# A Strassen scheme (seven block products for eight) for the gate and up projections of a decoder's FFN on one core

## The chip, the cores and the metric

The kernel runs on one core of a Trainium2 chip. The metric is device microseconds (us) of one execution, the median of several. The engines are named as the profile names them: PE (TensorE, the matmuls; PEld is its weight load), DVE (VectorE), ACT (ScalarE), POOL (GpSimd) and SP (which here only issues DMAs). PSUM is the memory that PE writes, SBUF the one that everything else lies in.

## The reference

One inference step of a two-layer decoder for 512 prompt tokens and 64 sample tokens, 576 columns in all, model width 1024. The change is in the FFN that closes each layer:

```python
D_MODEL = 1024
D_FF = -(-8 * D_MODEL // (3 * 256)) * 256        # 2816
def rmsnorm(x, g): ...
a = rmsnorm(x, norm_ffn[l])
x = x + (silu(a @ w_ffn_gate[l]) * (a @ w_ffn_up[l])) @ w_ffn_down[l]
```

Everything is float32.

## The kernel before

The activations stay in SBUF, features on the partitions: `h` is 8 chunks of 128 features by 576 columns. float32 accuracy is had from float32r matmuls by splitting: each operand is a high part H (ScalarE copies it to float32r) and a low part L (the remainder, subtracted on VectorE or GpSimd). A product W·X is three matmuls, WH·XH, WH·XL and WL·XH, added up in PSUM.

Weights come in blocks of 256 output columns by up to 8 chunks (`wblock`): two DMAs of 512 KB into `raw`, ACT writes `wh`, DVE or POOL (in turns, `remainder`, L303 and L305) writes `wl`. `dense` makes the next block while PE works on this one.

In the FFN the 576 columns are cut in 256 and 320. For the 256 the tile class `Halves` lays H and L side by side, so that WH·XH and WH·XL are one matmul of 512 columns (L239), followed by one of 256 for WL·XH (L241); `gather` (L222, L223) adds the two halves of PSUM up. The 320 take three matmuls (L235 to L237). `norm` makes the operand, chunk by chunk, while the matmuls of `dense` on `w_mem_o` are still adding to `h` (L374 `add_h`); 1/rms is multiplied onto the results later (`rs`, L284).

`ffn` goes through the 22 chunks of the hidden width in three groups of 8, 7 and 7. In a group, for each pair of chunks, a gate block (L284, L1043 Silu, L1044) and an up block (L1049, L1051, L1052) are made, which leave the operand `f` of the down projection; then `w_ffn_down` is applied to the group. So there are 11 gate and 11 up blocks of 256 columns in a layer, 44 in the kernel; here "block" always means one of these.

A framework turns the Python order into one instruction stream for each engine, puts semaphores where data or buffers ask for it, and shifts instructions by a plan of its own. On each engine they start in the order of the stream.

Of the kernel before, what the change touches and what calls it, by code (L numbers as in the profile page):

```python
# [94 lines left out]
def hybrid_step(ctx: ExitStack, tc: tile.TileContext, off, a, o):  # L95
# [104 lines left out]
    class Halves:  # L200
        def __init__(self, nm):
            self.t = [BIG(nm + x, FR) for x in "01"]

        def hl(self, c):
            return self.t[c // 4][:, 0:2048].rearrange("p (c x n) -> p c x n", x=2, n=256)[:, c % 4]

        def H(self, c, s0):
            return self.t[c // 4][:, 2048 + c % 4 * 320:2368 + c % 4 * 320] if s0 else self.hl(c)[:, 0]

        def L(self, c, s0):  # L210
            return self.t[c // 4][:, 3328 + c % 4 * 320:3648 + c % 4 * 320] if s0 else self.hl(c)[:, 1]

    both = [False]

    def bank(M, X, s0, n):
        p = ACC()
        return p[:M] if isinstance(X, Halves) and s0 == 0 and both[0] else p[:M, :n]

    def gather(po, n):
        if po.shape[1] > n:  # L220
            t = TMP("lo")[:po.shape[0], :n]
            nc.scalar.activation(t, po[:, n:n * 2], AF.Copy)  # L222
            last[0] = nc.vector.tensor_add(po[:, 0:n], po[:, 0:n], t)  # L223
        return po[:, 0:n]

    def products(po, W, X, k, ms, s0, n, nk):
        WH, WL = W[0][:, k, ms], W[1][:, k, ms]
        if isinstance(X, tuple):
            H, L = (x[:, k, s0:s0 + n] for x in X)
            nc.tensor.matmul(po, WH, H, start=k == 0, stop=False)  # L230
            nc.tensor.matmul(po, WH, L, start=False, stop=False)  # L231
            nc.tensor.matmul(po, WL, H, start=False, stop=k == nk - 1)  # L232
        elif po.shape[1] == n:
            H = X.H(k, s0)
            nc.tensor.matmul(po, WH, H, start=k == 0, stop=False)  # L235
            nc.tensor.matmul(po, WH, X.L(k, s0), start=False, stop=False)  # L236
            nc.tensor.matmul(po, WL, H, start=False, stop=k == nk - 1)  # L237
        else:
            nc.tensor.matmul(po.rearrange("p (x n) -> p x n", x=2), WH, X.hl(k), start=k == 0, stop=False,  # L239
                             skip_group_check=True)  # L240
            nc.tensor.matmul(po[:, 0:n], WL, X.H(k, 0), start=False, stop=k == nk - 1, skip_group_check=True)  # L241

    rs, rv, ssq = {}, {}, {}

    def norm(nm, l):
        X = Halves("a")
        for s0, n in HV:
            ssq[s0] = smp.tile([128, 320], FT, tag="ssq", name="ssq", bufs=2)[:, :n]
        for b in range(4):
            for s0, n in HV:  # L250
                s = slice(s0, s0 + n)
                acc = ssq[s0]
                for c in range(2 * b, 2 * b + 2):
                    g = vec(nm, l * 8 + c)
                    H = X.H(c, s0)
                    nc.scalar.activation(H, h[:, c, s], AF.Copy, scale=g)
                    nc.vector.scalar_tensor_tensor(X.L(c, s0), h[:, c, s], g, H, op0=OP.mult, op1=OP.subtract)  # L257
# [8 lines left out]
        normed[0] = X  # L266
        return X
# [22 lines left out]
    def plain(hi, lo, x):  # L290
        return [(hi, lo, x)]
# [15 lines left out]
    def wblock(w, k0, nk, m0, mc, load=None, order=None, into=None):  # L307
        WH, WL = into or [wp.tile([128, 8, 256], FR, tag=x, name=x) for x in ("wh", "wl")]
        for kk in range(0, nk, 4):
# [7 lines left out]
            remainder(WH[:, kk:kk + n, :mc], WL[:, kk:kk + n, :mc], raw[:, :n, :mc], order, into)  # L317
# [10 lines left out]
    def dense(w, X, k0, nk, m0, ncols, ev, load=None, order=None, fill=None, nxt=None, tick=None, hold=None):  # L328
        late = None
        W = ready.pop() if ready else wblock(w, k0, nk, m0, min(256, ncols), load, order)  # L330
        for b0 in range(0, ncols, 256):
            mc = min(256, ncols - b0)
            W0 = W
# [5 lines left out]
            for s0, n in HV:  # L339
                for mm in range(0, mc, 128):  # L340
# [3 lines left out]
                    if hold is not None and b0 == 0:  # L344
                        for k in range(nk - 1):
                            products(po, W0, X, k, ms, s0, n, nk)
                            pump(hold, 1)
# [6 lines left out]
                    if X is normed[0]:  # L354
                        rstd_cols(s0)
# [1501 lines left out]
```

## Time and profile before

| | us |
|---|---|
| median of 3 runs | 2116.62 (2116.26 to 2122.13) |
| the profiled execution, its own time | 2111.78 |
| its span, first to last instruction | 2109.9 |
| PE busy in the span | 2018.5 (96%) |
| DVE, ACT, POOL busy | 1111.7, 865.6, 801.0 |
| mean granted clock of PE | 0.984 of full |

A matmul's duration in a row runs from its start to its modelled end, and the next one starts long before that, so what a matmul costs is read from start to start. The two FFN stages are the stretches 596 to 1017 us and 1675.6 to 2099.7 us.

### The profile page before, as it was taken

The numbers are of one execution on the slowest core, as the hardware profiler recorded it, in microseconds if no ns is written. First come the engines' busy times: TensorE is split into PE (matmuls) and PEld (weight loads), VectorE is DVE, ScalarE is ACT, GpSimd is POOL, SyncE is SP. The second block draws the span as 40 slices with busy tenths as digits, with TensorE's granted clock in tenths as the row PEclk, the third lists the DMA queues.
The fourth block names the chain that finished last, engine by engine and source line by source line (L and its number), as shares of the span: only waits on it lengthen the run. The fifth ranks groups of instructions, "written<-read, shape, count | busy, mean of one in ns | idle before, by whom it ended". The sixth has DMA issues, their size and how long they took to land. (4 is left out here: it accounts for less than half of the span.)

```text
span 2109.9 us, 35813 instructions
## 1 busy us (share of the span) xinstructions
PE 2018.5 (96%) x14105; PEld 1817.6 (86%) x14105; DVE 1111.7 (53%) x2012; ACT 865.6 (41%) x1817; POOL 801.0 (38%) x752
## 2 busy tenths in 40 slices
PE   7999988999999999999969999999899999999998
PEld 6989846977899999999969977778887999999998
DVE  5478886544443333334535777765544433333344
ACT  5354555444333233133324547665444433232341
POOL 5354583422244234144302335563421443242342
PEclk9999998999999999999989999999999999999999
DMA  6545133255422222223344122312354222223232
GB/s 233 162 155 164 56 126 101 81 180 169 137 81 81 80 81 82 89 66 101 99 133 143 48 73 76 94 48 57 130 180 160 81 80 80 80 75 97 80 117 113
DMA packets 211156, 225.01 MB, mean 107 GB/s; under 512 B 13527, under 2 KB 191767, under 8 KB 210917
## 3 DMA queue, kind: packets, MB, share of 16 engines
q1 hardware_dynamic: 210989, 222.73, 33.0%
q8 instruction: 111, 1.82, 0.3%
q14 instruction: 56, 0.46, 0.1%
HBM read 210.04 MB, written 17.08 MB: 108 GB/s over the span
## 5 line engine op out<-in xcount | busy, mean ns | idle before, releaser
L235 PE MATMUL acc<-a,wh 128*128 128x320 f32 (+2 forms) x1616 | 501.4, 310 | 2.5 <-DVE hpb L500 2.5
L237 PE MATMUL acc<-a,wl 128*128 128x320 f32 (+2 forms) x1616 | 490.2, 303 | 0.0
L236 PE MATMUL acc<-a,wh 128*128 128x320 f32 (+2 forms) x1616 | 489.6, 303 | 0.0
L301 ACT ACTIVATE wh<-raw 128x1024 fp32r<-128x1024 f32 (+2 forms) x270 | 259.9, 986 | 384.1 <-PE acc L236 183.3
L305 POOL TENSOR_TENSOR wl<-raw,wh 128x1024 fp32r<-128x1024 f32 (+2 forms) x100 | 228.5, 2288 | 373.4 <-ACT wh L301 367.9
L235 PEld LDWEIGHTS acc<-a,wh 128*128 128x128 f32 (+1 forms) x1616 | 306.0, 189 | 9.4 <-issue 3.3
L236 PEld LDWEIGHTS acc<-a,wh 128*128 128x128 f32 (+1 forms) x1616 | 305.9, 189 | 3.0 <-issue 2.5
L237 PEld LDWEIGHTS acc<-a,wl 128*128 128x128 f32 (+1 forms) x1616 | 305.6, 189 | 3.1 <-issue 2.9
L303 DVE TENSOR_TENSOR wl<-raw,wh 128x1024 fp32r<-128x1024 f32 (+3 forms) x170 | 245.5, 1455 | 82.5 <-ACT wh L301 81.5
L239 PE MATMUL acc<-a,wh 128*128 128x512 f32 x704 | 251.2, 399 | 0.0
L241 PE MATMUL acc<-a,wl 128*128 128x256 f32 x704 | 197.7, 281 | 0.0
L374 DVE TENSOR_TENSOR h<-acc,h 128x256 f32<-128x256 f32 (+1 forms) x224 | 99.8, 448 | 171.0 <-PE acc L237 99.6
L239 PEld LDWEIGHTS acc<-a,wh 128*128 128x128 f32 x704 | 132.3, 188 | 30.5
L1044 POOL TENSOR_TENSOR sg<-sg,rs 128x256 f32<-128x256 f32 (+1 forms) x88 | 87.5, 996 | 153.8 <-ACT sg L1043 153.6
L263 POOL TENSOR_TENSOR ssq<-ssq,tmp 128x256 f32<-128x256 f32 (+1 forms) x84 | 80.3, 960 | 160.1 <-ACT tmp L262 158.7
L1052 POOL TENSOR_TENSOR f<-sg,f 128x256 fp32r<-128x256 f32 (+1 forms) x88 | 87.8, 998 | 133.0 <-ACT f L1051 133.0
L241 PEld LDWEIGHTS acc<-a,wl 128*128 128x128 f32 x704 | 133.1, 189 | 0.0
L1647 POOL TENSOR_TENSOR nar<-nar,f 128x512 f32<-128x512 f32 (+3 forms) x128 | 92.6, 746 | 87.3 <-DVE f L1645 53.0
L239 PE MATMUL acc<-f,wh 128*128 128x512 f32 x324 | 115.3, 398 | 0.0
L235 PE MATMUL acc<-f,wh 128*128 128x320 f32 x324 | 100.3, 310 | 0.0
L236 PE MATMUL acc<-f,wh 128*128 128x320 f32 x324 | 100.1, 309 | 0.0
L237 PE MATMUL acc<-f,wl 128*128 128x320 f32 x324 | 100.0, 309 | 0.0
(445 smaller groups left out, 4235.7 us busy)
## 6 DMA issues: line engine op xcount, KB each, us to landing
raw<-in_w_ffn_gate_dram SPq DMA_DIRECT2D x40, 512.0 KB
raw<-in_w_ffn_up_dram SPq DMA_DIRECT2D x40, 512.0 KB
ck<-in_cache_mem_k_dram SPq DMA_DIRECT2D x32, 512.0 KB
cv<-in_cache_mem_v_dram SPq DMA_DIRECT2D x32, 512.0 KB
raw<-in_w_ffn_down_dram SPq DMA_DIRECT2D x32, 512.0 KB
raw<-in_w_in_even_dram SPq DMA_DIRECT2D x20, 512.0 KB
raw<-in_w_mem_k_dram SPq DMA_DIRECT2D x16, 512.0 KB
raw<-in_w_mem_v_dram SPq DMA_DIRECT2D x16, 512.0 KB
```

Source lines behind the costliest of these rows:

```text
L235: nc.tensor.matmul(po, WH, H, start=k == 0, stop=False)
L236: nc.tensor.matmul(po, WH, X.L(k, s0), start=False, stop=False)
L237: nc.tensor.matmul(po, WL, H, start=False, stop=k == nk - 1)
L239: nc.tensor.matmul(po.rearrange("p (x n) -> p x n", x=2), WH, X.hl(k), start=k == 0, stop=False, skip_group_check=True)
L241: nc.tensor.matmul(po[:, 0:n], WL, X.H(k, 0), start=False, stop=k == nk - 1, skip_group_check=True)
L301: last[1] = nc.scalar.activation(hi, x, AF.Copy)
L303: nc.vector.tensor_sub(lo, x, hi)
L305: nc.gpsimd.tensor_sub(lo, x, hi)
L374: nc.vector.tensor_add(h[:, m, s0:s0 + n], p[:, x:x + n], h[:, m, s0:s0 + n])
L1044: nc.gpsimd.tensor_mul(t, t, rs[s0])
L1052: nc.gpsimd.tensor_sub(F.L(b0 + m, s0), t, H)
L1647: nc.gpsimd.tensor_tensor(P[:, x, :n], P[:, x, :n], f[:, x:x + 1].to_broadcast([128, n]), op=OP.mult)
```

## The change

For gate and up, a block's weights W (1024 by 256) and the operand X (1024 by 576) are cut in two along each side: A11, A12, A21, A22 of 512 by 128 (the first number counts halves of the output, the second halves of the 1024), and B11, B12, B21, B22 of 512 by 288. Seven products of sums (S1 to S4 of the weights, T1 to T4 of the operand, named in `RIGHT`) take the place of eight. Each product is 4 chunks by 3 matmuls of 288 columns, so a block is 84 matmuls. The seven go into three PSUM banks `A`, `B`, `E`, with copies p1, u2, s3 in between. `make` produces a block's weights in three portions while the block before it is multiplied; the operand's sums are made around the end of the `w_mem_o` matmuls and inside the first block. Everywhere else `Halves`, `gather` and the 512-column matmul are gone: a chunk of the down projection takes three matmuls of 256 and three of 320 columns. The groups of hidden chunks are now 8, 8 and 6.

```diff
-        for c0, nch in ((0, 8), (8, 7), (15, 7)):
-            F = Halves("f")
+        for c0, nch in ((0, 8), (8, 8), (16, 6)):
+            HH, HL = v8(BIG("fH", FR)), v8(BIG("fL", FR))
...
+    FH = 288
+    RIGHT = dict(A11="B11", S1="T1", S2="T2", A12="B21", S3="T3", A22="T4", S4="B22")
...
+        def second(self, cs):
+            for c in cs:
+                t2 = self.t2[:, c]
+                nc.vector.scalar_tensor_tensor(t2, h[:, c + 4, FH:T], self.g(c + 4), self.t1[:, c],
+                                               op0=OP.mult, op1=OP.add)
+                H, L = (t[:, c] for t in self.X["T2"])
+                nc.scalar.activation(H, t2, AF.Copy)
+                nc.vector.tensor_sub(L, t2, H)
...
+        def make(self, W, w, m0):
...
+            def pair(t, i, nm, x, eng):
...
+                nc.scalar.activation(H, x, AF.Copy)
+                eng.tensor_sub(L, x, H)
...
+            nc.vector.tensor_add(s1, a21, a22)
+            t = self.slot()
+            pair(t, 0, "A11", a11, nc.vector)
+            pair(t, 1, "S1", s1, nc.vector)
+            yield 1
+            nc.vector.tensor_sub(s2, s1, a11)
+            t = self.slot()
+            pair(t, 0, "S2", s2, nc.vector)
+            pair(t, 1, "A12", a12, nc.gpsimd)
...
+            nc.vector.tensor_sub(s3, a11, a21)
+            nc.vector.tensor_sub(s4, a12, s2)
+            yield 1
+            t = self.slot()
+            pair(t, 0, "S3", s3, nc.vector)
+            pair(t, 1, "A22", a22, nc.gpsimd)
...
+            nc.scalar.activation(v[:, 0], s4, AF.Copy)
+            nc.vector.tensor_sub(v[:, 1], s4, v[:, 0])
...
+        def product(self, po, W, nm, start, stop):
+            (WH, WL), (H, L) = W, self.X[nm]
+            for k in range(4):
+                nc.tensor.matmul(po, WH[:, k], H[:, k], start=start and k == 0, stop=False, skip_group_check=True)
+                nc.tensor.matmul(po, WH[:, k], L[:, k], start=False, stop=False, skip_group_check=True)
+                nc.tensor.matmul(po, WL[:, k], H[:, k], start=False, stop=stop and k == 3, skip_group_check=True)
...
+        def block(self, out, then):
...
+            mul(A, "A11", True, False)
+            nc.scalar.activation(p1, A, AF.Copy)
...
+            mul(B, "S2", True, False)
+            nc.vector.tensor_add(B, B, p1)
+            nc.scalar.activation(u2, B, AF.Copy)
+            if fresh:
+                mul(A, "A12", False, True)
+            else:
+                mul(E, "S1", True, False)
+            ahead()
+            mul(B, "S3", False, False)
+            nc.scalar.activation(s3, B, AF.Copy)
+            c22 = TMP("sg")[:, :FH]
+            nc.vector.tensor_add(c22, E, s3)
+            if fresh:
+                for s0 in (0, FH):
+                    rstd_cols(s0)
+            else:
+                mul(A, "A12", False, True)
+            ahead()
+            mul(B, "A22", False, True)
+            out(0, 0, A)
+            mul(E, "S4", False, True)
+            out(1, 0, B)
+            out(1, FH, c22, True)
+            nc.vector.tensor_add(E, E, u2)
+            out(0, FH, E)
...
+                def out_up(m, s0, p, own=False):
                     t = sg[m, s0]
...
+                    (nc.gpsimd if own else nc.vector).tensor_mul(t, p, t)
+                    x = HH[:, b0 + m, s0:s0 + FH]
+                    nc.scalar.activation(x, t, AF.Copy)
+                    nc.gpsimd.tensor_sub(HL[:, b0 + m, s0:s0 + FH], t, x)
...
```

`fresh` is true in a layer's first block alone.

What the streams hold at three places follows; the line numbers are those of the file that each belongs to. VectorE before, one gate block and the start of the up block behind it in the first group:

```order
L223 TENSOR_TENSOR acc<-acc,lo 128x256
L284 TENSOR_TENSOR sg<-acc,rs 128x256
L223 TENSOR_TENSOR acc<-acc,lo 128x256
L284 TENSOR_TENSOR sg<-acc,rs 128x256
L284 TENSOR_TENSOR sg<-acc,rs 128x320 x2
L303 TENSOR_TENSOR wl<-raw,wh 128x1024
L223 TENSOR_TENSOR acc<-acc,lo 128x256
L1049 TENSOR_TENSOR sg<-acc,sg 128x256
```

VectorE of the changed kernel, from the last two results of an up block through the gate block that follows it in the first group. L1199 is E + u2, L1230 the up result, L1119, L1130 and L1124 the weight sums s1, s3 and s2 of the next block, L1177 is B + p1, L1131 is s4, L1115 and L1139 are low parts, L1187 is c22:

```order
L1199 TENSOR_TENSOR acc<-acc,gu 128x288
L1230 TENSOR_TENSOR sg<-acc,sg 128x288
L1119 TENSOR_TENSOR s_6613<-raw 128x512
L1130 TENSOR_TENSOR s_6653<-raw 128x512
L1124 TENSOR_TENSOR s_6613<-s_6613,raw 128x512
L1177 TENSOR_TENSOR gb<-gb,gu 128x288
L1115 TENSOR_TENSOR wl<-s_6613,wl 128x512
L1131 TENSOR_TENSOR s_6653<-raw,s_6613 128x512
L1115 TENSOR_TENSOR wh<-s_6613,wh 128x512
L1139 TENSOR_TENSOR s4w<-s_6653,s4w 128x512
L1187 TENSOR_TENSOR sg<-acc,gu 128x288
```

The one or two weight instructions of 1024 in a block have become nine of 512, and three of them stand ahead of L1177.

GpSimd before, from an up block into the next gate and up blocks (L1044 multiplies the gate by `rs`, L1052 makes the low part of `f`, L305 that of a weight):

```order
L1044 TENSOR_TENSOR sg<-sg,rs 128x256 x2
L1044 TENSOR_TENSOR sg<-sg,rs 128x320 x2
L305 TENSOR_TENSOR wl<-raw,wh 128x1024
L1052 TENSOR_TENSOR f_6189<-sg,f_6189 128x256 x2
L1052 TENSOR_TENSOR f_6189<-sg,f_6189 128x320 x2
```

GpSimd of the changed kernel, a gate block and the up block behind it (L1225 multiplies the gate by `rs`, L1230 is the one up result of POOL, L1233 makes the low part of `f`, L1115 that of A12 and A22):

```order
L1225 TENSOR_TENSOR sg<-sg,rs 128x288 x2
L1115 TENSOR_TENSOR wl<-raw,wl 128x512
L1225 TENSOR_TENSOR sg<-sg,rs 128x288 x2
L1115 TENSOR_TENSOR wl<-raw,wl 128x512
L1230 TENSOR_TENSOR sg<-sg 128x288
L1233 TENSOR_TENSOR fL<-sg,fH 128x288 x2
L1115 TENSOR_TENSOR wh<-raw,wh 128x512
L1233 TENSOR_TENSOR fL<-sg,fH 128x288 x2
L1115 TENSOR_TENSOR wh<-raw,wh 128x512
```

A gate block has four instructions of 288 and two of 512 elements, an up block five and two, where either had four of 256 and 320 and, in two blocks of three, one of 1024.

VectorE of the changed kernel in the first block of layer 0, behind the last residual add (L340). L1061 to L1084 make T2, B21, T3, T4 and B22 of the last feature chunk (L1084 of two chunks), the other names are those above:

```order
L340 TENSOR_TENSOR h<-acc,h 128x320
L1115 TENSOR_TENSOR wh<-s_6148,wh 128x512
L1061 SCALAR_TENSOR_TENSOR tsum<-h,vt,tsum 128x288
L1029 SCALAR_TENSOR_TENSOR x_5923<-h,vt,x_5923 128x288
L1072 SCALAR_TENSOR_TENSOR tmp<-h,vt,tsum 128x288
L1029 SCALAR_TENSOR_TENSOR x_5924<-h,vt,x_5924 128x288
L1065 TENSOR_TENSOR x_5923<-tsum,x_5923 128x288
L1119 TENSOR_TENSOR s_6326<-raw 128x512
L1076 SCALAR_TENSOR_TENSOR x_5924<-tmp,x_5924 128x288
L1084 SCALAR_TENSOR_TENSOR tmp<-h,vt,tsum 128x288 x2
L1177 TENSOR_TENSOR gb<-gb,gu 128x288
```

Before, one L257 (the low part of the last chunk's 320 columns) and two weight instructions followed that add; now all that a first block needs of the last chunks stands there, in front of L1177.

## Rows read from the trace of the kernel before

**Rows 1.** The profile page: busy time, share of the span, instructions.
```profile
PE 2018.5 (96%) x14105; PEld 1817.6 (86%) x14105; DVE 1111.7 (53%) x2012; ACT 865.6 (41%) x1817; POOL 801.0 (38%) x752
```

**Rows 2.** Two windows, the FFN stages: PE, PEld, DVE, ACT, POOL busy, clock, DMA.
```profile
596.00:1017.00 421.00, 421.00 (x2662) 396.41 (x2661) 169.94 (x271) 134.86 (x238) 155.39 (x128) 1.00 0.27 85
1675.60:2099.70 424.10, 423.88 (x2686) 399.05 (x2685) 167.83 (x274) 128.66 (x223) 149.39 (x126) 1.00 0.28 89
```

**Rows 3.** PE's timeline around the start of layer 0's FFN: start, duration, instruction.
```profile
574.78 0.28 PE L230 MATMUL acc<-cH,wh 128*128 128x256 f32 x1
574.90 0.28 PE L231 MATMUL acc<-cL,wh 128*128 128x256 f32 x1
...
595.77 0.31 PE L231 MATMUL acc<-cL,wh 128*128 128x320 f32 x1
595.91 0.31 PE L232 MATMUL acc<-cH,wl 128*128 128x320 f32 x1
596.06 0.39 PE L239 MATMUL acc<-a,wh 128*128 128x512 f32 x1
596.29 0.28 PE L241 MATMUL acc<-a,wl 128*128 128x256 f32 x1
```

**Rows 4.** DVE's timeline in four blocks of layer 0.
```profile
645.79 0.49 DVE L1049 TENSOR_TENSOR sg<-acc,sg 128x320 f32<-128x320 f32 x1 [2.15 <-PE acc L237]
...
653.69 0.42 DVE L223 TENSOR_TENSOR acc<-acc,lo 128x256 f32<-128x256 f32 x1
...
662.88 1.23 DVE L303 TENSOR_TENSOR wl<-raw,wh 128x1024 fp32r<-128x1024 f32 x1 [0.39 <-ACT wh L301]
...
671.17 0.49 DVE L1049 TENSOR_TENSOR sg<-acc,sg 128x320 f32<-128x320 f32 x1 [2.15 <-PE acc L237]
...
689.57 2.23 DVE L303 TENSOR_TENSOR wl<-raw,wh 128x1024 fp32r<-128x1024 f32 x1 [1.69 <-ACT wh L301]
```

**Rows 5.** POOL's timeline in the same four blocks.
```profile
652.62 1.89 POOL L1052 TENSOR_TENSOR f<-sg,f 128x320 fp32r<-128x320 f32 x1
...
684.93 0.88 POOL L1044 TENSOR_TENSOR sg<-sg,rs 128x320 f32<-128x320 f32 x1 [1.95 <-ACT sg L1043]
688.31 2.40 POOL L305 TENSOR_TENSOR wl<-raw,wh 128x1024 fp32r<-128x1024 f32 x1 [2.50 <-ACT wh L301]
690.66 1.87 POOL L1044 TENSOR_TENSOR sg<-sg,rs 128x320 f32<-128x320 f32 x1
```

**Rows 6.** Timelines of DVE and POOL: weight instructions of 512 elements.
```profile
814.73 0.69 DVE L303 TENSOR_TENSOR wl<-raw,wh 128x512 fp32r<-128x512 f32 x1
827.47 1.29 DVE L303 TENSOR_TENSOR wl<-raw,wh 128x512 fp32r<-128x512 f32 x2
815.30 1.28 POOL L305 TENSOR_TENSOR wl<-raw,wh 128x512 fp32r<-128x512 f32 x1 [2.59 <-ACT wh L301]
```

**Rows 7.** Groups by shape: count, busy us, mean ns of one, idle before.
```profile
L303 DVE TENSOR_TENSOR wl<-raw,wh 128x512 fp32r<-128x512 f32 x20 | 15.7, 815 | 2.1 <-ACT wh L301 2.1
L257 DVE SCALAR_TENSOR_TENSOR a<-h,vt,a 128x320 fp32r<-128x320 f32 x48 | 47.1, 988 | 13.7 <-ACT a L256 13.6
L139 ACT ACTIVATE cos<-cs 128x256 f32<-128x256 f32 x8 | 3.1, 385 | 11.0 <-PE cs L927 5.9 <-DVE cos L141 5.1
```

**Rows 8.** PE's timeline early in the program, a wait of PE and what follows.
```profile
22.81 0.50 PE L413 MATMUL mp<-wl,memx 128*128 128x512 f32 x1 [0.69 <-POOL wl L305]
23.15 0.39 PE L411 MATMUL mp<-wh,memx 128*128 128x512 f32 x1
```

**Rows 9.** PE's timeline where the first group's down projection starts.
```profile
699.65 0.31 PE L237 MATMUL acc<-a,wl 128*128 128x320 f32 x1
699.80 0.39 PE L239 MATMUL acc<-f,wh 128*128 128x512 f32 x1
```

**Rows 10.** Two windows before the FFN, columns as in rows 2.
```profile
440.00:500.00 60.00, 56.78 (x460) 48.33 (x459) 27.55 (x54) 23.79 (x57) 11.81 (x15) 1.00 0.54 174
280.00:360.00 80.00, 69.95 (x556) 42.10 (x556) 62.41 (x95) 44.52 (x96) 47.32 (x42) 0.85 0.36 121
```

More of the change, by code (lines that the diff above doesn't have):

```diff
@@ L198, in rstd_rows @@
         return r
[L200 to L241, printed above, removed]
     rs, rv, ssq = {}, {}, {}
     def norm(nm, l):
-        X = Halves("a")
+        H, L = BIG("aH", FR), BIG("aL", FR)
+        H, L = v8(H), v8(L)
         for s0, n in HV:
@@ L265, in norm @@
         rv.clear()
-        normed[0] = X
-        return X
+        normed[0] = H
+        return H, L
     def rstd_cols(s0):
@@ L316, in wblock @@
                 load(raw, k0 + kk, m0)
-            remainder(WH[:, kk:kk + n, :mc], WL[:, kk:kk + n, :mc], raw[:, :n, :mc], order, into)
+            remainder(WH[:, kk:kk + n, :mc], WL[:, kk:kk + n, :mc], raw[:, :n, :mc], order, into and dve)
         return WH, WL
@@ L363, in dense @@
                 for f, x in held:
-                    products(*f)
+                    f(nk - 1)
                     if late is not None:
-                        ev(*late[:3], late[3] if ev is add_h else gather(late[3], late[2]))
+                        ev(*late)
                     late = x
@@ L369, in dense @@
                 fill()
-        ev(*late[:3], late[3] if ev is add_h else gather(late[3], late[2]))
+        ev(*late)
     def add_h(m, s0, n, p):
-        for x in range(0, p.shape[1], n):
-            nc.vector.tensor_add(h[:, m, s0:s0 + n], p[:, x:x + n], h[:, m, s0:s0 + n])
+        nc.vector.tensor_add(h[:, m, s0:s0 + n], p, h[:, m, s0:s0 + n])
     def mem_load():
@@ L1027, in ffn @@
+    def ffn(l, fast, nxt):
+        wd = a["w_ffn_down"][l]
         kept = []
@@ new lines, in out_up @@
+                    x = HH[:, b0 + m, s0:s0 + FH]
+                    nc.scalar.activation(x, t, AF.Copy)
+                    nc.gpsimd.tensor_sub(HL[:, b0 + m, s0:s0 + FH], t, x)
+                fast.block(out_gate, [])
+                if b0 + 2 == nch:
+                    later, fast.blocks = fast.blocks, []
+                    fast.block(out_up, [down()])
+                    fast.blocks = later
+                    if not ready:
+                        pump([down()], 1)
+                else:
+                    fast.block(out_up, [])
@@ L1068, in ffn, with tick @@
+            if c0 < 16 or l == 0:
+                n_ = [0]
+                def tick():
+                    n_[0] += 1
+                    if c0 < 16 and n_[0] == 50:
+                        fast.take()
+                    if c0 < 16 and n_[0] in (54, 58):
+                        pump(fast.G[1], 1)
+                dense(wd, (HH, HL), c0, nch, 0, 1024, add_h, nxt=nxt if c0 == 16 else None, tick=tick)
         if l == 0:
-            both[0] = False
             return
         out = [final(*HV[0])]
-        W = [first, ready.pop()]
+        W = [ready.pop(), wblock(wd, c0, nch, 256, 256)]
```

207 lines of the change are left out of this document (163 added, 44 removed).

## The prediction

> **What bounds the kernel now.** First I read the page: PE is busy for 96% of the span [rows 1]. Then the windows of the two FFN stages: PE is busy in 421.00 of 421.00 us and 423.88 of 424.10 us, at the full clock, while DVE is busy 170 us, POOL 155 us and ACT 135 us [rows 2]. So in the stages that the change rewrites, PE alone sets the time, and a shorter list of matmuls is worth all that it saves, as long as nothing else falls into PE's way. The timelines come next: PE passes from the projection before into the FFN without a gap (595.91, 596.06) [rows 3], and from an up block into the down projection (699.65, 699.80) [rows 9]. The reader is to see there that every operand is ready ahead of time.
>
> The last view is that of DVE and POOL side by side. A weight remainder of 1024 elements takes DVE 1.23 us at 662.88 and 2.23 us at 689.57 [rows 4]. In the second case POOL had been running since 688.31 and ended at 690.71 [rows 5]; DVE ended at 691.80, 1.09 us later. The POOL instruction that started at 690.66 took 1.87 us where its like takes 0.88: it ended 0.73 us after DVE did [rows 5]. So the two take turns: each waits for the other's end, and pays then some 0.15 us less than its time alone. DVE instructions with an operand in PSUM don't wait: L223 took 0.42 us at 653.69, inside POOL's 652.62 to 654.51 [rows 4, 5]. Before, that costs nothing, since DVE's idle time covers it.
>
> **The change, term by term.** The sum is made against the profiled execution, 2111.8 us (span 2109.9), 4.8 us under the median of the runs.
>
> 1. *Matmuls of gate and up.* A block now: two blocks lie between 645.79 and 671.17 [rows 4], so 12.69 us each. After: 84 matmuls of 288 columns. The pace from start to start is 0.120 us for 256 columns and 0.29 / 2 = 0.145 us for 320 [rows 3], so 0.133 us for 288 and 11.2 us for the block. The saving is 1.5 us, times 44 blocks: **-66 us**. Seven products for eight would be 1/8 of the time if all of it went by columns; it nearly does.
>
> 2. *Waits inside a block with its next weights to make* (36 of 44: not the first of a layer, nor the six at a group's end). A product takes 12 x 0.133 = 1.6 us. S2, the second, has its result at 3.36 us after the block's start (its last matmul starts at 3.07 and lasts 0.29, between 0.28 and 0.31 [rows 3]). S1 follows until 4.8 us; then S3 adds to the bank that S2 left, and must wait until DVE has added p1 to it (L1177, 0.46 us, between 0.42 and 0.49 [rows 4]) and ACT has copied u2 (0.41 us from 0.385 for 256 [rows 7]). So L1177 may start about 0.5 us after S2's result, at 3.8 to 3.9 us, before S3 waits. Ahead of it in DVE's stream stand the last results of the block before (two of 0.46 us, the first of which can start at about 0.2 us), then three weight sums. One of 512 elements takes 0.69 us alone, and two in a row 1.29 us [rows 6], 0.60 us each. Without POOL, L1177 starts at 0.2 + 2 x 0.42 + 3 x 0.60 = 2.9 us, and PE never waits. But all three sums read SBUF twice, and just then POOL has its queue of gate products or remainders of the block before: 1.28 us for 512 elements [rows 6], and from that and 0.88 for 320 [rows 5] about 0.81 us for 288. A turn of POOL costs DVE 0.66 us (0.81 less 0.15) or 1.13 us (1.28 less 0.15). Lower end: no turn, 0. With two short turns L1177 starts at 4.2 us and S3 waits 0.4 us; with one long and two short it starts at 5.35 us and S3 waits 1.5 us. Upper end: all turns of the block are waited out, 2.0 us (worked out below). POOL has six or seven instructions per block, DVE ten that take turns, so a turn ahead of each sum is the likely case; I take the middle of 0.4 and 1.5, rounded up for the later waits on s3 and c22: 1.05 us. After a wait PE's next start comes 0.34 us later [rows 8] where 0.23 us is its pace [rows 3]: another 0.1 us. 36 x 1.15 = **+41 us** (0 to 72). What is late next is all behind S3 in the same bank; the group's last block makes no weights and has nothing to wait for.
>
> 3. *The first block of a layer.* Before, one low part followed the last residual add, and `norm` ran under the matmuls. Now everything of the last two feature chunks comes behind late residual adds, and the first block's S2, S3, A22 and S4 need it. Behind the last add DVE has eight weight instructions (0.60 us), eight of 288 (0.45 us, 0.99 us as a mean with POOL's turns in it for 320 [rows 7]) and L1177: 8.8 us alone. Six or so POOL turns lie in it (0.66 to 1.13 us each, 5 us). c22 comes then, S4 waits for it, and in PE's stream the 1/rms matmuls, which wait for DVE and POOL, stand there too. PE has 9.6 us of products ahead of S4. So 3 us late if few turns are waited for, 10 us if all are and the adds themselves come late behind older DVE work. I take 9, near the upper end because the two streams have these instructions in turn: **+18 us** for two layers (6 to 20).
>
> 4. *The down projection.* A chunk: 0.23 + 0.12 + 3 x 0.146 = 0.79 us before, 3 x 0.120 + 3 x 0.146 = 0.80 us after, 352 of them: **+2 us**. At each of six group starts, POOL has its up product and four remainders (5 x 0.81 = 4.0 us) bunched at the block's end, where they were spread before; the remainder of the last chunk is needed 7 chunks x 0.36 = 2.5 us into the first 256 columns. They begin some 1 us before the block's end at best, so the wait is 0 to 4 us; 2 us: **+12 us** (0 to 24).
>
> 5. *At no cost.* ACT's eight halves instead of two wholes per block: half busy, some 7 us of each 11. DMA: the same two transfers of 512 KB per block, at a share of 0.27 [rows 2]. The copies p1, u2, s3 save the `gather` pair. If PE did stand for that cover, each us of a block would be 44 us.
>
> Sum: -66 + 41 + 18 + 2 + 12 = **+7 us**, 2119 us for a profiled execution, **2124 us** for the median.
>
> Beside the rows on the turns stands the Trainium skill, page "SBUF — State Buffer", section "SBUF: two separate sides": VectorE and GpSimd share a port pair, an exclusive lock held for a whole instruction, and a DVE instruction with two SBUF inputs needs it against a GpSimd one that reads SBUF. This speaks against the change, and the trace agrees on who waits (2.23 us for 1.23). Of the price it differs: the page has the blocked side going on some 115 ns after the other's end, for a DMA's descriptors; the trace has it 0.14 us cheaper than alone. By the page's figure three turns a block would cost 36 x 3 x 0.25 = 27 us more (an estimate), 2151 us.
>
> **The rivals.**
>
> *PE does not wait in the blocks* (faster). If POOL's work falls behind L1177, or DVE runs far enough ahead, term 2 is at most 0.4 us a block, terms 3 and 4 shrink alike to 10 and 6: -66 + 14 + 10 + 2 + 6 = -34, 2083 us. For it: DVE alone needs 2.9 us where 3.9 are allowed. Against it: POOL's queue is fullest just there. It decides at a mean wait of (66 - 18 - 2 - 12) / 36 = 0.94 us: below, the kernel gets faster. Chance 0.2.
>
> *DVE and POOL become the bound* (slower). If DVE waits out every turn, a gate block takes 9 x 0.60 + 7 x 0.38 of its own (0.38 is 0.46 at the pace that 0.60 has to 0.69) and 4 x 0.66 + 2 x 1.13 of POOL's: 13.0 us, an up block 13.3 us, 2.0 us over PE's 11.2: -66 + 72 + 18 + 2 + 12 = +38, 2155 us. Against it: a third of DVE's instructions read PSUM and can run in a turn of POOL. Chance 0.18.
>
> *The clock falls in the longer waits.* With PE busy 56.78 of 60 us it stayed at 1.00, with 69.95 of 80 us it was 0.85 [rows 10]. Waits of 1 us in 12 look like the first; the first blocks may see a fall to 1.2 GHz, some 5 us in all. Chance 0.05 that it decides. That the seven products aren't done is excluded: the stream has 44 x 84 = 3696 of them.
>
> **How the numbers follow.** The forecast's case (waits of 0.7 to 1.5 us) has 0.57 and by its terms 2106 to 2142 us. The faster rival has 0.2, the slower ones 0.23. To leave out no more than 2 in 10, the range is 2104 to 2148. A change under 0.3% (2110 to 2123) can't be told from none by a measurement of this kernel. The lower third of my case falls in there or just below, so: faster 0.2, the same 0.28, slower 0.52.
>
> **What would show it.** A steady block from one A11 to the next 11.2 us plus a wait of PE ahead of S3, put down to ACT's u2 copy, with L1177 late; DVE's 512-element instructions at a mean near or above 0.82 us [rows 7]; first blocks near 20 us; PE's busy share in the stages near 90% at the full clock. I am wrong if PE's gaps before S3 are under 0.9 us on average, or if the groups' starts show no wait.

## The result, and the profile after

| | before | changed |
|---|---|---|
| median of 5 runs, us | 2116.26 (2115.05 to 2122.13) | 2134.65 (2134.22 to 2139.0) |
| the profiled execution, its own time | 2111.78 | 2134.22 |
| its span | 2109.9 | 2132.5 |

The changed kernel is slower: the ratio is 1.0087, with a 95% interval of 1.007 to 1.0104. That is 18.4 us between the medians; 7 us were forecast, and 2134.65 lies inside the range of 2104 to 2148. One of the six runs of e10 below took 2198.09 us at a granted clock of 0.839, where the others have 0.974 to 0.979, and is left out of its row.

The page's busy line, which answers to [rows 1]:

```profile
PE 1986.8 (93%) x14641; PEld 1821.7 (85%) x14641; DVE 1369.5 (64%) x2366; ACT 970.5 (46%) x2105; POOL 910.0 (43%) x838
```

PE has 536 matmuls more and is busy 32 us less, and still the span is 22.6 us longer: time has gone into waits. The windows of the two FFN stages (first and third row) and of the stretch between them, with the columns of [rows 2]:

```profile
596.00:1023.40 427.40, 400.91 (x2930) 393.82 (x2930) 289.01 (x433) 184.50 (x373) 209.63 (x173) 0.99 0.30 89
1023.40:1690.80 667.40, 624.62 (x4785) 547.95 (x4785) 408.99 (x910) 323.99 (x768) 238.09 (x272) 0.97 0.33 99
1690.80:2122.30 431.50, 404.51 (x2956) 398.18 (x2954) 286.70 (x432) 177.26 (x358) 207.11 (x171) 0.98 0.28 89
```

Before, PE had hardly a gap in these stages; now it stands still for some 27 us of each. DVE is busy 289 us in the first where it had 170. The stages are 13.8 us longer together than in the trace of before (427.4 and 431.5 against 421.0 and 424.1 us, read from the first gate matmul to the matmul behind the last down one).

Where PE waits inside a block is read from its timeline: the end of S1, and S3 behind it, in a gate block that starts at 656.2 us.

```profile
660.73 0.29 PE L1146 MATMUL acc<-x,wh 128*128 128x288 f32 x1
660.86 0.29 PE L1147 MATMUL acc<-x,wh 128*128 128x288 f32 x1
662.15 0.40 PE L1145 MATMUL gb<-x,wh 128*128 128x288 f32 x1 [0.99 <-ACT gu L1178]
662.38 0.29 PE L1146 MATMUL gb<-x,wh 128*128 128x288 f32 x1
```

From 660.86 to 662.15 are 1.29 us where the pace is 0.13. The wait is put down to ACT's copy u2 (L1178), which in turn waited for DVE's B+=p1 (L1177). DVE's timeline up to that instruction, in the same block:

```profile
657.06 0.45 DVE L1199 TENSOR_TENSOR acc<-acc,gu 128x288 f32<-128x288 f32 x1
657.62 0.46 DVE L1230 TENSOR_TENSOR sg<-acc,sg 128x288 f32<-128x288 f32 x1
658.00 0.84 DVE L1119 TENSOR_TENSOR s<-raw 128x512 f32<-128x512 f32 x1
658.76 1.30 DVE L1130 TENSOR_TENSOR s<-raw 128x512 f32<-128x512 f32 x1
659.99 1.29 DVE L1124 TENSOR_TENSOR s<-s,raw 128x512 f32<-128x512 f32 x1
661.20 0.45 DVE L1177 TENSOR_TENSOR gb<-gb,gu 128x288 f32<-128x288 f32 x1
```

and POOL's, at the same time:

```profile
656.56 1.74 POOL L1115 TENSOR_TENSOR wh<-raw,wh 128x512 fp32r<-128x512 f32 x1
658.26 2.47 POOL L1233 TENSOR_TENSOR fL<-sg,fH 128x288 fp32r<-128x288 f32 x2
```

B+=p1 starts 5.0 us after the block's start. Each of the last two sums takes 1.30 us for 0.69 alone: one turn of POOL, which itself needs 2.47 us for two instructions of 0.81. The block's length over many blocks is read from three starts, those of the first and the last block of the second group and of the down projection behind it:

```profile
757.12 0.29 PE L1145 MATMUL ga<-x,wh 128*128 128x288 f32 x1
...
842.93 0.30 PE L1145 MATMUL ga<-x,wl 128*128 128x288 f32 x1
...
854.13 0.28 PE L307 MATMUL acc<-fH,wh 128*128 128x256 f32 x1
```

The last block, which has no gate or up weights to make, takes 11.20 us; the seven ahead of it (842.93 - 757.12) / 7 = 12.26 us. The 34 blocks of that kind in the kernel (not the first two of a layer, nor the last of a group) have this mean, gate blocks 12.37, up blocks 12.10 us.

The first block of layer 0 took 22.65 us. Its two longest waits, from PE's timeline, and two windows, of the stretch behind the longest wait and of the second group's blocks:

```profile
605.87 0.40 PE L1145 MATMUL gb<-x,wh 128*128 128x288 f32 x1 [1.63 <-ACT gu L1178]
613.96 0.80 PE L194 MATMUL rsb<-ident,var 128*128 128x128 f32 x2 [4.10 <-POOL var L188]
```

```profile
612.00:617.40 5.40, 3.44 (x15) 3.44 (x16) 2.85 (x5) 0.18 (x1) 2.89 (x3) 0.51 0.55 170
757.10:854.10 97.00, 91.61 (x674) 89.77 (x673) 80.25 (x117) 52.49 (x109) 56.83 (x49) 1.00 0.31 92
```

PE waited 4.1 us for POOL's 1/rms. Its input, a DVE instruction (L187), stood in DVE's queue behind weight sums until 611.44 us; L188 itself began at 612.60 us, behind the low parts of A12 and A22. Behind the wait PE ran at the lower clock level (1.2 of 2.4 GHz; mean granted 0.51). The waits of 1 us in the steady blocks leave the clock at 1.00.

### The profile page after: what moved, and what is told of

It reads as the page before. It is cut to its first block, busy times and chain, and to the rows that moved or that the text cites. A ratio compares the mean times of both kernels' runs of the same rounds, so it can differ in the third digit from the quotient of the medians.

```text
span 2132.5 us, 37543 instructions
## 1 busy us (share of the span) xinstructions
PE 1986.8 (93%) x14641; PEld 1821.7 (85%) x14641; DVE 1369.5 (64%) x2366; ACT 970.5 (46%) x2105; POOL 910.0 (43%) x838
## 5 line engine op out<-in xcount | busy, mean ns | idle before, releaser
L307 PE MATMUL acc<-aH,wh 128*128 128x256 f32 (+2 forms) x912 | 284.6, 312 | 2.5 <-DVE hpb L466 2.5
L263 POOL TENSOR_TENSOR wl<-raw,wh 128x1024 fp32r<-128x1024 f32 (+1 forms) x68 | 160.9, 2371 | 269.6 <-ACT wh L259 255.3
L309 PE MATMUL acc<-aH,wl 128*128 128x256 f32 (+2 forms) x912 | 274.3, 301 | 0.0
L308 PE MATMUL acc<-aL,wh 128*128 128x256 f32 (+2 forms) x912 | 273.2, 300 | 0.0
L259 ACT ACTIVATE wh<-raw 128x1024 fp32r<-128x1024 f32 (+1 forms) x174 | 168.0, 992 | 202.7 <-PE acc L308 90.4
L308 PE MATMUL acc<-fL,wh 128*128 128x320 f32 (+1 forms) x608 | 182.0, 299 | 8.2 <-POOL fL L1233 8.2
L340 DVE TENSOR_TENSOR h<-acc,h 128x320 f32<-128x320 f32 (+1 forms) x176 | 79.5, 454 | 166.9 <-PE acc L309 151.2
L307 PE MATMUL acc<-fH,wh 128*128 128x320 f32 (+1 forms) x608 | 181.6, 299 | 0.8 <-ACT fH L1232 0.8
L309 PE MATMUL acc<-fH,wl 128*128 128x320 f32 (+1 forms) x608 | 181.3, 298 | 0.0
L307 PEld LDWEIGHTS acc<-aH,wh 128*128 128x128 f32 (+1 forms) x912 | 174.7, 192 | 7.4 <-issue 3.3
L308 PEld LDWEIGHTS acc<-aL,wh 128*128 128x128 f32 (+1 forms) x912 | 174.8, 192 | 2.9 <-issue 2.5
L309 PEld LDWEIGHTS acc<-aH,wl 128*128 128x128 f32 (+1 forms) x912 | 174.5, 191 | 3.1 <-issue 2.9
L1115 POOL TENSOR_TENSOR wl<-raw,wl 128x512 fp32r<-128x512 f32 x44 | 66.9, 1521 | 114.9 <-ACT wl L1114 114.9
L1225 POOL TENSOR_TENSOR sg<-sg,rs 128x288 f32<-128x288 f32 x88 | 89.1, 1034 | 60.5 <-ACT sg L1224 60.5
L1115 POOL TENSOR_TENSOR wh<-raw,wh 128x512 fp32r<-128x512 f32 x44 | 66.4, 1510 | 97.6 <-ACT wh L1114 97.6
L1233 POOL TENSOR_TENSOR fL<-sg,fH 128x288 fp32r<-128x288 f32 x88 | 97.1, 1114 | 23.5 <-ACT fH L1232 22.8
```

What stands on the lines that cost most here:

```text
L259: last[1] = nc.scalar.activation(hi, x, AF.Copy)
L263: nc.gpsimd.tensor_sub(lo, x, hi)
L307: nc.tensor.matmul(po, WH[:, k, ms], H[:, k, s], start=k == 0, stop=False)
L308: nc.tensor.matmul(po, WH[:, k, ms], L[:, k, s], start=False, stop=False)
L309: nc.tensor.matmul(po, WL[:, k, ms], H[:, k, s], start=False, stop=k == nk - 1)
L340: nc.vector.tensor_add(h[:, m, s0:s0 + n], p, h[:, m, s0:s0 + n])
```

## The experiments

Each is timed against runs of the kernel before that were made beside it, so kernels are compared by their ratios. The column "stages" is the sum of the two FFN stages in the profiled execution, "steady" the mean of the 34 blocks named above, "starts" the sum of PE's waits in the first 40 matmuls of the six down projections (start to start, less the pace).

| kernel | median us | ratio, interval | stages | steady | starts |
|---|---|---|---|---|---|
| before, profiled twice | 2116.3 to 2119.7 | 1 | 845.1, 845.6 | 12.69 | 0 |
| changed, profiled twice (e9) | 2134.65 | 1.0087, 1.007 to 1.0104 | 858.9, 857.3 | 12.26 | 13.3, 13.8 |
| e1 | 2105.3 | 0.9946, 0.9927 to 0.9965 | 832.4 | 11.62 | 8.9 |
| e2 | 2065.1 (one) | | 790.3 | 11.20 | 0.2 |
| e3 | 2135.44 | 1.0087, 1.0061 to 1.0113 | 853.7 | 12.26 | 10.3 |
| e5 | 2100.62 | 0.9911, 0.9894 to 0.9928 | 822.8 | 11.45 | 10.8 |
| e6 | 2092.82 | 0.9876, 0.9857 to 0.9895 | 814.1 | 11.23 | 11.3 |
| e7 | 2090.71 | 0.9873, 0.985 to 0.9896 | 807.7 | 11.24 | 7.5 |
| e8 | 2078.2 | 0.9806, 0.9788 to 0.9824 | 800.4 | 11.23 | 2.9 |
| e10 | 2129.91 | 1.0064, 1.0044 to 1.0083 | 860.4 | 12.26 | 14.1 |
| e11 | 2074.02 | 0.9796, 0.9778 to 0.9814 | 799.4 | 11.24 | 2.9 |

**Is it the order of VectorE's stream, or turns with GpSimd?** The first two kernels take away one half each of the mechanism that the prediction named for the waits ahead of S3.

e1 queues what is made ahead behind B+=p1:

```diff
-            nc.vector.tensor_add(B, B, p1)
+            added = nc.vector.tensor_add(B, B, p1)
...
-                if self.G:
-                    pump(self.G[1], 1)
-                else:
-                    pump(then, 1)
+                with tc.issue_after(added.ins):
+                    if self.G:
+                        pump(self.G[1], 1)
+                    else:
+                        pump(then, 1)
```

> The changed kernel with the weight sums and all else that a block makes for the next block queued on VectorE behind B+=p1. If PE's wait ahead of S3 comes from the order of VectorE's stream (three sums with turns of GpSimd ahead of B+=p1), the wait falls from a mean of 1.06 us to under 0.3 us, blocks take 11.2 to 11.5 us for 12.26, and the kernel gains 20 to 36 us. If VectorE and GpSimd together are the bound (rival: their work fills the block), the wait only moves to the first products of the next block, blocks stay at 12 us or more, and the time changes by under 8 us.

The order theory holds: the mean wait ahead of S3 fell from 0.94 to 0.23 us over the pace (with the restart behind it 1.06 us before), the steady block to 11.62 us, a little over the 11.5 expected, and the kernel beats the one before. DVE's 512-element instructions still take a mean of 0.89 us (0.93 before), so the turns are still there. The rest of the wait sits in up blocks (0.67 us in most) and in the groups' last blocks, which grew from 11.20 to 12.4 us. One of these, the last of layer 0, took 16.10 us: its c22 stood behind a DVE copy that waited 6.55 us for a transfer (e7 and e8 come to it). In the others another late step shows: ACT's timeline and DVE's, in the last block of the first group (it starts at 688.2 us):

```profile
692.37 0.43 ACT L1225 ACTIVATE sg<-sg 128x288 f32<-128x288 f32 x1
692.71 0.39 ACT L1169 ACTIVATE gu<-ga 128x288 f32<-128x288 f32 x1
```

```profile
693.12 0.47 DVE L1178 TENSOR_TENSOR gb<-gb,gu 128x288 f32<-128x288 f32 x1 [1.24 <-ACT gu L1169]
```

ACT's copy p1 (here L1169) stands behind a Silu of the block before, which waits for DVE's last result (at 691.43 us, 0.46 us long); so B+=p1 (here L1178) waits for ACT.

e2 takes POOL out of the gate and up work of the blocks (it keeps the remainders of the down weights) and leaves the order of the sums as it was (`None` in `pair`, for A22 too, stands for a copy on ScalarE in place of the low part):

```diff
-            pair(t, 1, "A12", a12, nc.gpsimd)
+            pair(t, 1, "A12", a12, None)
...
-                    nc.gpsimd.tensor_mul(t, t, rs[s0])
+                    nc.scalar.activation(t, t, AF.Copy)
...
-                    (nc.gpsimd if own else nc.vector).tensor_mul(t, p, t)
+                    nc.vector.tensor_mul(t, p, t)
...
-                    nc.gpsimd.tensor_sub(HL[:, b0 + m, s0:s0 + FH], t, x)
+                    nc.scalar.activation(HL[:, b0 + m, s0:s0 + FH], t, AF.Copy)
```

> In the gate and up blocks all work of GpSimd is replaced: the low parts of A12, A22 and f and the product with rs by copies on ScalarE, its up product by one on VectorE; so these operands hold other values. The order of VectorE's sums ahead of B+=p1 stays. If the turns with GpSimd make B+=p1 late, a 512-element VectorE instruction falls from a mean near 1 us to 0.6 to 0.7 us, the wait ahead of S3 goes to 0 to 0.2 us and a steady block takes 11.2 to 11.4 us; with the down projection's starts about 50 us less, 2080 to 2090 us. If the order alone makes it late, the wait stays at 0.7 us or more and blocks at 12 us.

Every steady block takes 11.20 us and PE waits for nothing in them. The one run is 69.6 us under the changed kernel's median, more than the 50 expected: the first blocks fell too, from 22.65 and 22.94 to 16.06 and 15.96 us. DVE's groups by shape (count, busy, mean ns), first of the changed kernel, then of e2, where the same sums are L1133, L1127 and L1122:

```profile
L1130 DVE TENSOR_TENSOR s<-raw 128x512 f32<-128x512 f32 x44 | 51.0, 1159 | 0.0
L1124 DVE TENSOR_TENSOR s<-s,raw 128x512 f32<-128x512 f32 x44 | 49.7, 1130 | 0.0
L1119 DVE TENSOR_TENSOR s<-raw 128x512 f32<-128x512 f32 x44 | 37.4, 850 | 12.1 <-DMA raw<-in_w_ffn_gate_dram 12.1
```

```profile
L1133 DVE TENSOR_TENSOR s<-raw 128x512 f32<-128x512 f32 x44 | 31.3, 712 | 0.0
L1127 DVE TENSOR_TENSOR s<-s,raw 128x512 f32<-128x512 f32 x44 | 31.3, 712 | 0.0
L1122 DVE TENSOR_TENSOR s<-raw 128x512 f32<-128x512 f32 x44 | 30.2, 685 | 12.7 <-DMA raw<-in_w_ffn_gate_dram 12.7
```

With the order unchanged and no turns, the wait is gone; with the turns unchanged and another order, most of it is gone. So the wait needed both. e2 also shows what the scheme is worth when GpSimd isn't in its way: 790 us for the stages, 55 us less than before, with the work left out that POOL did there.

**The starts of the down projection.** e3 gives DVE the low parts of f in a group's last up block (`nc.vector` for `nc.gpsimd` where `b0 + 2 == nch`).

> The changed kernel with the low parts of f made on VectorE instead of GpSimd in the last up block of each group. If GpSimd's bunched remainders hold up the down projection, PE's waits at the six starts (13.2 us in the trace, and some 4 us more at the lower clock behind them) fall to under 4 us and the kernel gains 10 to 16 us. If VectorE is as late with them, or the wait is for ScalarE's high parts, less than 5 us.

The theory falls: the time is the same, the waits at the starts fell by 3 us only. The rows show why. First PE's wait at the first start of the changed kernel and POOL's timeline ahead of it, then POOL's and ACT's in e3:

```profile
708.46 0.39 PE L308 MATMUL acc<-fL,wh 128*128 128x256 f32 x1 [1.19 <-POOL fL L1233]
```

```profile
698.15 3.45 POOL L263 TENSOR_TENSOR wl<-raw,wh 128x1024 fp32r<-128x1024 f32 x1 [2.05 <-PE acc L1147]
701.56 0.81 POOL L1230 TENSOR_TENSOR sg<-sg 128x288 f32<-128x288 f32 x1
702.93 0.82 POOL L1233 TENSOR_TENSOR fL<-sg,fH 128x288 fp32r<-128x288 f32 x1 [0.56 <-ACT fH L1232]
```

```profile
699.39 3.45 POOL L263 TENSOR_TENSOR wl<-raw,wh 128x1024 fp32r<-128x1024 f32 x1 [2.05 <-PE acc L1147]
```

```profile
706.85 1.06 ACT L259 ACTIVATE wh<-raw 128x1024 fp32r<-128x1024 f32 x1 [1.48 <-DMA raw<-in_w_ffn_down_dram]
707.81 0.43 ACT L1232 ACTIVATE fH<-sg 128x288 fp32r<-128x288 f32 x1
```

At this start it is not the remainders of f but those of the next weights: L263, 1024 elements of the down weights, holds POOL for 3.45 us ahead of the up product, and ACT's copy of the same weights, which waits for its transfer, stands ahead of the high part of f. The third start of the changed kernel (at 979.2 us), with 4.1 of the 13.3 us the longest, has mainly another cause. DVE's two up products stand behind a copy for layer 1 that waits for its own transfer:

```profile
980.33 0.43 DVE L1371 COPY cn<-cn 128x512 f32<-128x512 f32 x1 [4.72 <-DMA cn<-in_cache_nsa_cmp_k_dram]
980.67 0.45 DVE L1230 TENSOR_TENSOR sg<-ga,sg 128x288 f32<-128x288 f32 x1
```

e7 and e8 below test these.

**Is the rest of the program steady?** Between the two FFN stages the change adds only the operand's sums for layer 1, at the end of that stretch; the first two traces differ there by 8.8 us.

> The kernel before, profiled once more. The stretch between the two FFN stages, which the change does not rewrite, took 658.6 us in the trace of before and 667.4 us in that of the changed kernel. If the 8.8 us come from the instruction streams (or from other addresses), it takes 658 to 660 us again. If it is spread between executions, it takes 661 to 667 us, and the difference of the medians (18.4 us) rather than that of the two profiled spans (22.6 us) is what the change costs.

> The changed kernel, profiled once more. If its FFN stages are steady and the rest of the program varies between executions, the two stages take 427 to 428 us and 431 to 432 us again, with the same waits ahead of S3 to 0.05 us, while the stretch between them moves by some us from 667.4 us. If the stages vary too, the comparison of terms by one trace each is worth less than it looks.

The windows, of e4 (the kernel before) and of e9 (the changed one), in the order first stage, stretch between, second stage:

```profile
592.40:1013.40 421.00, 421.00 (x2663) 396.51 (x2662) 169.87 (x271) 134.82 (x238) 155.36 (x128) 1.00 0.28 85
1013.40:1682.10 668.70, 623.61 (x4785) 546.50 (x4785) 396.60 (x890) 320.37 (x758) 238.03 (x272) 0.97 0.33 100
1682.10:2106.70 424.60, 424.22 (x2688) 399.11 (x2686) 168.61 (x274) 128.50 (x223) 149.47 (x126) 1.00 0.29 89
```

```profile
597.50:1025.00 427.50, 401.48 (x2930) 394.61 (x2929) 288.73 (x433) 184.36 (x374) 209.25 (x173) 0.99 0.30 89
1025.00:1692.60 667.60, 623.75 (x4786) 547.28 (x4785) 407.95 (x910) 323.61 (x768) 237.84 (x272) 0.97 0.33 99
1692.60:2122.40 429.80, 402.59 (x2954) 396.05 (x2953) 286.21 (x432) 176.79 (x358) 206.97 (x171) 0.99 0.29 89
```

The stages of before repeat to 0.5 us, those of the changed kernel to 1.7 us (its waits ahead of S3 to 0.01 us), so their difference is 11.7 to 13.8 us. The stretch between moved by 10 us within one program, from 658.6 to 668.7 us in the kernel before, beyond both ranges of e4, on the side of a spread between executions. In the changed kernel it hardly moved (667.4 and 667.6 us), and e9's second stage came 1.2 us under its range. One place where the two programs differ in both pairs of traces is in the attention of layer 1: from the first matmul of a transpose (L1847) to the next wait at a mask matmul (L1820) PE takes 5.9 us in both traces of the kernel before and 11.2 us in both of the changed one. There the framework's plan has put the factor f of a softmax (L1833) behind a maximum (L1641):

```profile
1248.71 1.21 DVE L1641 TENSOR_REDUCE mx<-csz 64x8 f32<-64x1024 f32 x1
1249.84 0.14 DVE L1833 TENSOR_TENSOR f<-f,kvA 128x2 f32<-128x2 f32 x1
```

PE waits 1.1 and 1.6 us for POOL's product with f, and the clock falls (0.72 over 1249 to 1261 us). The longer wait:

```profile
1253.20 0.47 PE L1847 MATMUL ntp<-ident,nar 128*128 128x128 f32 x1 [1.59 <-POOL nar L1835]
```

e10 exchanges the two in the changed kernel (`tc.issue_after` on the maximum):

> The changed kernel with one pair of VectorE's instructions exchanged, in the attention of layer 1, which the change does not rewrite: the factor f of a softmax stands ahead of a 1.2 us maximum again, as in the stream of the kernel before. Both traces of the changed kernel lose 4.2 us of PE at this place against both traces of the kernel before (two waits for GpSimd's product with f, then half clock). If the exchange made by the framework's plan is the cause, the waits go, 3 to 5 us of the stretch between the FFN stages come back, and the median falls from 2134.5 to 2129.5 to 2132 us. If the loss has another cause (addresses, transfers), the waits at this place stay and the median stays within 1.5 us.

At this place PE takes 6.65 us in e10 for 11.2, and the longer wait is gone, so the exchange is the cause there. In the length of the whole stretch it doesn't show: 666.6 us in e10's trace, for 667.4 and 667.6. In the ratio it shows as 1.0064 for 1.0087, 4.9 us; the intervals overlap, so that the program gains from it is not shown.

**Clearing the way, step by step.** e5 builds on e1: the last result of a block is traced behind the next block's p1, so that p1 doesn't queue behind it.

```diff
-            nc.scalar.activation(p1, A, AF.Copy)
+            early = nc.scalar.activation(p1, A, AF.Copy)
+            if self.tail:
+                with tc.issue_after(early.ins):
+                    self.tail.pop()()
...
+            def tail():
+                nc.vector.tensor_add(E, E, u2)
+                out(0, FH, E)
```

> The kernel of e1 (sums behind B+=p1), and the last result of a block (E + u2 and what follows) traced behind the copy p1 of the next block on ScalarE. In e1 a Silu that waits for VectorE's last result stood ahead of that copy, and VectorE waited 30.9 us in all for it ahead of B+=p1. If this is what was left of PE's wait ahead of S3 (0.67 us in every second block, 1.1 us in the six last blocks of the groups), it goes to under 0.1 us, blocks take 11.2 to 11.35 us, and the kernel gains 12 to 20 us over e1. If VectorE is full anyway (rival), the wait moves to other products and the gain is under 6 us.

The wait ahead of S3 is 0.00 in the steady blocks, but 0.17 us appear ahead of S4, whose bank waits for DVE's c22, and the last blocks still take 12.07 us. The ratio falls by 0.35 points, 7.4 us: between the two theories. The late p1 was the cause of the wait ahead of S3 in the steady blocks (the last blocks keep 0.77 us of it in four of six), and DVE was also near full (81.56 us busy of the 92.3 us of the second group).

e6 takes four instructions of POOL out of each gate block: 1/rms is multiplied onto the result of the down projection.

```diff
+    def add_f(m, s0, n, p):
+        for x, w in ((0, 256),) if s0 == 0 else ((0, 32), (32, 288)):
+            f0 = FH if s0 + x >= FH else 0
+            nc.vector.tensor_mul(p[:, x:x + w], p[:, x:x + w], rs[f0][:, s0 + x - f0:s0 + x - f0 + w])
+        add_h(m, s0, n, p)
...
-                    nc.gpsimd.tensor_mul(t, t, rs[s0])
```

> The kernel of e5, with the second 1/rms no longer multiplied onto the gate by GpSimd (four instructions of a gate block) but onto the results of the down projection by VectorE, from PSUM. If turns with GpSimd still delay VectorE after e5, blocks go to 11.2 us and the six starts of the down projection lose little of their waits: 0 to 10 us less than e5. If e5 has nothing left to gain in the blocks, or VectorE's more work in the down projection delays h, within 4 us of e5 or slower.

Blocks take 11.23 us, the ratio falls by another 0.35 points, and the mean of DVE's 512-element instructions from 0.93 to 0.85 us. That fits the turns as what was left; that the gate's results are ready sooner by the same edit is not separated from it. The starts kept their waits.

e7 puts the matmuls for 1/rms behind S4 in a layer's first block, and makes the low part of the down weights that a group starts with on DVE (`wblock(wd, c0, nch, 0, 256, low=True)`).

> The kernel of e6 with two more edits at other places. In the first block of a layer, the matmuls that spread 1/rms over the partitions stand behind S4 on PE, instead of inside A22 where PE waited 4.4 us for them and ran at half clock behind: first blocks fall from 19 to 20 us to 14.5 to 17 us. And VectorE instead of GpSimd makes the low parts of the down weights that a group starts with, so that the 1024-element remainder of GpSimd (3.45 us) no longer stands ahead of its up product: if that is what makes fL late, the waits at the six starts fall from some 10 us to under 4 us. Together 8 to 18 us less than e6. If the starts wait for ScalarE's high parts behind a weight whose transfer is late, the waits at the starts stay above 6 us, and the gain is the first blocks' alone, 4 to 9 us.

It missed: the ratio is that of e6. Two of the starts where POOL's remainder of 1024 elements stood lost their wait and a third half of it (11.3 to 7.5 us in all), but the first blocks gained nothing: with their second blocks they take 61.7 us for 62.4. The stages are 6.4 us shorter in its trace, but the stretch between them is 4.2 us longer (677.4 us for 673.2), so the time doesn't show it. After e1, PE's wait for 1/rms was only 0.6 us in the first block of layer 0; the expectation was made from the changed kernel, where it was 4.1 us. In other groups POOL's remainder of the second portion of weights still came ahead of f's low parts (L1256), and in the last block of layer 0 DVE stood still for a transfer that only layer 1 needs:

```profile
952.52 0.43 DVE L1394 COPY cn<-cn 128x512 f32<-128x512 f32 x1 [3.80 <-DMA cn<-in_cache_nsa_cmp_k_dram]
952.86 0.45 DVE L1198 TENSOR_TENSOR sg<-acc,gu 128x288 f32<-128x288 f32 x1
```

```profile
832.17 2.41 POOL L263 TENSOR_TENSOR wl<-raw,wh 128x1024 fp32r<-128x1024 f32 x1
834.53 3.35 POOL L1256 TENSOR_TENSOR fL<-sg,fH 128x288 fp32r<-128x288 f32 x3
```

c22 (L1198) behind that copy made S4 wait 1.7 us. e8 gives DVE all low parts of the down weights and queues the copy behind the last up result.

> The kernel of e7 with VectorE making the low parts of all down weights (GpSimd still made those of the second portion in three groups of six, 1.3 to 2.4 us ahead of the last low parts of f), and with VectorE's copies of cached rows for layer 1 queued behind the last up result of layer 0 (in e7 one of them waited 3.8 us for its transfer, with c22 of the last block behind it). If these are what is left, the waits at the starts fall from 7.5 us in all to under 2 us, the last block of layer 0 takes 11.2 to 11.5 us for 13.2, and the kernel gains 6 to 11 us over e7 (2080 to 2085 us). If fL is late by its own chain (E + u2, up product, high part, low part), the waits stay above 5 us and the gain is 2 to 4 us.

Both causes hold, each at its place: five of the six starts wait 0 to 0.2 us, the last block of layer 0 takes 11.20 us, the stages are 7.3 us shorter. The third start keeps 2.7 us, where ACT's copy of down weights waits 3.51 us for its transfer ahead of the high part of f. The ratio fell by 0.67 points, 14 us, more than the stages explain. In these two traces the stretch between them differs as well, 677.4 us in e7's and 667.9 in e8's; whether e8's edit did that is not shown, since that stretch moves by 10 us by itself.

> The same exchange in the kernel of e8 (2078.2 us), as the last version: 3 to 5 us less, 2073 to 2076 us, if the exchange is the cause; within 1.5 us of e8 if not.

Its 2074.02 us are 4.2 us less, but the ratio moved by 0.1 points only, which these runs don't tell from none; the stretch between the stages took 668.8 us for e8's 667.9. It stands as the last version: 2% faster than the kernel before, as e8 is.

## Why the prediction came out as it did

The direction, the sign of the sum and the place of the largest cost were right; the sum was too small. Term by term, against the first pair of traces:

| term | forecast | measured | from |
|---|---|---|---|
| 1 matmuls | -66 | -65.6 | 44 x (12.69 - 11.20) |
| 2 waits ahead of S3 | +41 | +40.2 | 34 x 1.06, and two second blocks 2.0 and 2.2 over 11.2 (their longest waits are ahead of A22) |
| 3 first blocks | +18 | +18.3 | 22.65 + 22.94 - 22.4, less 4.9 in before |
| 4 down projection | +14 | +20.9 | 302.7 us in six stretches for 281.8 |
| elsewhere | 0 | +5.3 at one place | 11.2 us for 5.9 in the attention of layer 1 |

1. *Right.* A block that waits for nothing takes 11.20 us.

2. *Right, mechanism and size.* The wait is ahead of S3, put down to u2, with B+=p1 late behind three sums that take turns. The turn was priced at 0.66 us over the instruction's own time; the rows show 1.30 us for 0.69, 0.61 more. DVE's 512-element instructions have a mean of 0.93 us, over the 0.82 that were named. The faster rival decides at a mean of 0.94 us, and the wait with its restart was 1.06: the outcome hung on some tenths of a microsecond, as e1 shows from the other side. Over all 36 blocks that the prediction counts, the mean wait ahead of S3 is 0.90 us (0.38 and 0.12 in the two second blocks), just at the 0.9 us under which it called itself wrong. (The 2106 to 2142 us that it gives its own case don't follow from waits of 0.7 to 1.5 us alone: these give 2111 to 2140.)

3. *Right in size, half right in cause.* (Before, the first eight blocks of a layer took 103.7 and 104.2 us, where eight times 12.69 are 101.5: 4.9 us together.) DVE's queue and the turns were named; the longest wait, 4.1 us, is that of the 1/rms matmuls, named there without a price, and the lower clock behind it was priced at nothing in the forecast's case. That the size came out is in part luck.

4. *The step that failed.* It said that at a start "POOL has its up product and four remainders bunched at the block's end". The waits came to 13.3 us where 12 were forecast, but by another cause, so the size was luck: POOL's remainder of the down weights and ACT's copy of them stood ahead, and at the third start a copy of DVE's that waited for a transfer (e3 falsified the prediction's cause, e7 and e8 showed these). The up block's end had been looked at, not what is made there for the next stages. The other 7.6 us are the pace and the clock. The pace is 51.33 us for eight chunks in e8, where nothing waits, against 50.76 before: 0.07 us for each of 44 chunks, 3.1 us. The prediction has 2 there, though its own 0.788 and 0.798 us a chunk give 3.5. The 4.5 us that are left were priced at nothing: behind the longest waits, at three of the six starts, some 55 matmuls start up to 0.21 us apart for 0.12, as here behind a wait of 2.35 us. PE's rows, then a window, with a granted clock of 0.53:

```profile
1806.15 0.41 PE L309 MATMUL acc<-fH,wl 128*128 128x256 f32 x1
1806.36 0.41 PE L307 MATMUL acc<-fH,wh 128*128 128x256 f32 x1
```

```profile
1805.00:1808.00 3.00, 3.00 (x16) 3.00 (x16) 0.42 (x1) 0.00 (x0) 0.49 (x1) 0.53 0.54 180
```

5. *Missed.* No term stood for work that the change doesn't touch. The framework's plan moved an instruction 220 us behind the stage, which cost 5.3 us at that place. With the 11.7 to 13.8 us from the stages that would be 17.0 to 19.1 us, for 18.4 measured. But the stretch between the stages moves by 10 us by itself, and its length did not fall in e10, so that this place makes up the difference stays open.

Of the rivals, "DVE and POOL become the bound" didn't come: DVE was busy 80.25 of 97.0 us in the second group, and e1 gained by order alone. Beside this stands what the Trainium skill says (page "SBUF — State Buffer", section "SBUF: two separate sides"): whichever of DVE, with two SBUF inputs, and GpSimd, reading SBUF, starts first holds the shared pair for its whole instruction. The trace agrees that one waits for the other: two of the sums shown take 1.30 us beside POOL, and the means without it in e2 are 0.69 to 0.71 us. On the price it differs: by the 115 ns that the page has from the other side's end, measured there for a DMA's descriptors, a sum with one turn would take 0.69 + 0.81 + 0.12 = 1.62 us (an estimate from the page); the row has 1.30.

## What to carry to other kernels

Fewer matmuls shorten a PE-bound stage only by what the other engines can keep ahead of; read the streams of the engines that make the operands, and ask of each instruction on PE's path what stands ahead of it in its queue, for the next stage's weights too. Work made ahead belongs behind the result that PE waits for, and a prefetch whose transfer may be late belongs behind everything that PE needs soon. Two elementwise engines that read SBUF together are not two engines: when e6 took four instructions of a gate block from one, the other's 512-element instructions fell from a mean of 0.93 to 0.85 us. Order and turns in the blocks, and then what stood ahead at the starts of the down projection, made most of the difference between 0.9% slower and 2% faster.

## What the runs showed of the hardware

- A wait of 1 us in each 12 us leaves PE's granted clock at 1.00 over 97 us; one of 4.1 us was followed by a stretch with a mean of 0.51, one of 2.35 us by a stretch of 0.53.
- A 512-element VectorE instruction with two SBUF inputs took 1.30 us beside GpSimd's work and 0.69 us alone; one of 288 elements with an operand in PSUM took 0.45 us in the same block.
- The stages under study repeat to 0.5 us in the kernel before, while the stretch between them took 658.6 us in one execution and 668.7 us in the next; a cost of a few microseconds in that stretch can't be read from one trace.
